# Two of the four sums of weight blocks in the FFN's first product, made by accumulating DMA transfers

## The chip, the core and the metric

The kernel runs on one core of a Trainium2 chip. The metric is device time: the microseconds of one execution of the whole program. Three executions of the kernel before were timed, and one more was taken by the hardware profiler.

## The reference

One layer of a hybrid trunk: 512 latent tokens and 256 context tokens of width 2048 go through a modulated RMS norm, one projection, two groups of heads (a gated token mixer and a bidirectional gated linear attention), an output projection, and a SwiGLU feed-forward network (FFN). Everything is in float32. The change lies in the FFN's first product, `h @ w_in`:

```python
def swiglu(h, w_in, w_out):
    a, b = jnp.split(h @ w_in, 2, axis=-1)
    return (jax.nn.silu(a) * b) @ w_out
...
    f_x = swiglu(modulate(rms_norm(x, g_pre_ffn), mod_x[3], mod_x[4]), w_ffn_in, w_ffn_out)
```

Here h is 512 x 2048 and w_in is 2048 x 11264 (two halves of 5632 columns).

## The kernel before

**Engines and queues.** TensorE multiplies; ScalarE casts, evacuates and evaluates activations; VectorE subtracts and adds; nearly all loads are issued by SyncE (SP) through `load` (L193). GpSimd does 22 small fills in the whole program and issues no transfer. The order of the instructions in each engine's queue is not written out by hand: a scheduler works it out at build time from the dependencies, the program order and its own estimates of what each instruction takes. Every queue then runs strictly in that order, and an instruction whose input is not there holds what is behind it.

**Precision.** A float32 product is made of three matmuls in a reduced format (`three`, L298): each operand is split into a hi part (a cast, ScalarE) and a lo part (source minus hi, VectorE), and hi·hi, hi·lo and lo·hi are summed in PSUM. `parts` (L988) makes both parts of a 128 x 1024 tile, the cast on L992 and the subtraction on L993; three buffers (tags wh, wl) hold them.

**The FFN's first product** is cut into 11 groups of columns (`ffn_group`, L1136), f0 to f10 in the names of the tiles. A group takes 512 columns of each half. The 2 x 2 block product (tokens x depth times depth x column halves) is made with seven products instead of eight, in the manner of Strassen and Winograd: `product(p, q, ...)` (L1118), p = 1 to 7, each over the four quarters q = 0 to 3 of half the depth. One `product` call is 12 matmuls of 512 columns. The left operands (sums of blocks of h, `SP[p][q]`) are made once, before and during group 0, by `make_top` and `make_rest` (L1082, L1089). The right operands are blocks of the weights, `blk(i, j, q, t)` (L1141): half i of the depth, half j of the columns, quarter q, loaded by `wide` (L996) as one transfer of 512 KB, 128 partitions x 1024 floats, in rows of 2 KB.

The stages of a group, by the letter in the names of their hi and lo parts:

- a: blocks (0,0) are loaded into four X tiles (tag X, four buffers) and go into product 1.
- b: blocks (1,0), into R tiles (tag R, four buffers), go into product 2.
- c: blocks (0,1) are loaded into R tiles, VectorE adds each to X[q] (L1169), and the sum goes into product 5.
- d: blocks (1,1) are loaded and added to X[q] (L1174), for product 6.
- e: blocks (1,0) are loaded again and added to X[q] (L1182), for product 4.
- z, y: for each q, block (1,1) is loaded as z and goes into product 3; block (0,1) is loaded as y, VectorE adds z to it (L1191), and the sum goes into product 7. Both are R tiles.

So there are four sums per group, each made four times (q), and all four are made by VectorE: L1169, L1174, L1182 and L1191, 16 adds per group. An R or X tile's buffer is used again when its last reader has finished; the next load into it waits for that. In steady state the hi and lo parts are made some two products ahead of TensorE, as their three buffers come free. Between the stages VectorE combines the accumulators (`vtt`, L1132), and at the end of a group the result is transposed and stored by ScalarE's queue.

During group 0 the pumps `bg` and `bgm` interleave other work: the residual of the mixer (L1034: its RMS, ending in the newton steps of L183 to L185, and the scaling `yo`, L1051) and the operands of the later products (`make_rest`, with the tiles S3 to S7 and h2f).

Of the kernel before, what the change touches and what calls it, by code (L numbers as in the profile page):

```python
# [15 lines left out]
ALU = mybir.AluOpType  # L16
AX = mybir.AxisListType

P = 128
# [72 lines left out]
def trunk_kernel(ctx, tc, cmat, cmask, x, c, ctxt, c_ctx, w_mod, b_mod, g_pre_mix, g_post_mix, g_pre_ffn,  # L92
                 g_post_ffn, w_in, ln_g, ln_b, w_s, b_s, wd2_f, bd_f, wd2_b, bd_b, out_g, w_out, w_ffn_in,
                 w_ffn_out, out):
    nc = tc.nc
    V, S, T, G = nc.vector, nc.scalar, nc.tensor, nc.gpsimd
# [12 lines left out]
    def bank(name, main=True):  # L109
        return pm.tile([P, 512], F32, tag="mm" if main else "ms", bufs=6 if main else 2, name=name)  # L110

    def slot(name, dt=F32, shape=(P, 512)):
        return s2.tile(list(shape), dt, tag="s2", bufs=NS, name=name)
# [26 lines left out]
    def rstd(ss, n, scale, name, eng=None):  # L140

        v = cp.tile([P, n], F32, tag=f"rv{n}", bufs=2, name=name + "v")
        r = cp.tile([P, n], F32, tag=f"rr{n}", bufs=4 if n == 1 else 2, name=name + "r")
        t = cp.tile([P, n], F32, tag=f"rt{n}", bufs=2, name=name + "t")
        V.tensor_scalar(out=v, in0=ss, scalar1=scale, scalar2=EPS, op0=ALU.mult, op1=ALU.add)
        V.tensor_scalar(out=r.bitcast(I32), in0=v.bitcast(I32), scalar1=-0.5, scalar2=float(0x5F3759DF), op0=ALU.mult,
                        op1=ALU.add)
        for _ in range(3):
            if eng is None:
                newton(v, r, t)  # L150
            else:
                eng.tensor_tensor(out=t, in0=r, in1=r, op=ALU.mult)
                eng.tensor_tensor(out=t, in0=t, in1=v, op=ALU.mult)
                eng.tensor_scalar(out=t, in0=t, scalar1=-0.5, scalar2=1.5, op0=ALU.mult, op1=ALU.add)
                eng.tensor_tensor(out=r, in0=t, in1=r, op=ALU.mult)
        return r
# [4 lines left out]
    def rstd_exp(ss, n, name):  # L161

        s1 = cp.tile([P, n], F32, tag=f"s{n}", bufs=4, name=name + "s")
        v = cp.tile([P, n], F32, tag=f"rv{n}", bufs=2, name=name + "v")
        r = cp.tile([P, n], F32, tag=f"rr{n}", bufs=4 if n == 1 else 2, name=name + "r")
        t = cp.tile([P, n], F32, tag=f"rt{n}", bufs=2, name=name + "t")
        V.tensor_reduce(out=s1, in_=ss, axis=AX.X, op=ALU.add)
        S.activation(r, s1, AF.Ln, bias=eps, scale=1.0 / D)
        S.activation(r, r, AF.Exp, scale=-0.5)
        V.tensor_scalar(out=v, in0=s1, scalar1=1.0 / D, scalar2=EPS, op0=ALU.mult, op1=ALU.add)  # L170
        newton(v, r, t)
        return r

    def rstd_sum(ss, name, eng=None):

        s1 = cp.tile([P, 1], F32, tag="s1", bufs=4, name=name + "s")
        V.tensor_reduce(out=s1, in_=ss, axis=AX.X, op=ALU.add)
        return rstd(s1, 1, 1.0 / D, name, eng)
# [102 lines left out]
    def pump():  # L281
        bg.step()
        bgm.step()
# [406 lines left out]
    for o in (0, 512):  # L690
        n = min(512, len(LEVELS) * P - o)
# [260 lines left out]
    for g in range(2):  # L952
# [10 lines left out]
        for b, ev in enumerate(evs):  # L963
            k = g * 4 + b
# [14 lines left out]
    def fslot(name, dt=F32):  # L979
        return fp.tile([P, 512], dt, tag="f", bufs=NF, name=name)  # L980

    def chain_tile(name):
        return st2.tile([P, 1024], F32, tag="X", bufs=4, name=name)

    def raw2(name):
        return st2.tile([P, 1024], F32, tag="R", bufs=4, name=name)

    def parts(src, name):  # L988

        wh = st2.tile([P, 1024], F32R, tag="wh", bufs=3, name=name + "h")  # L990
        wl = st2.tile([P, 1024], F32R, tag="wl", bufs=3, name=name + "l")
        S.copy(wh, src)  # L992
        V.tensor_tensor(out=wl, in0=src, in1=wh.bitcast(F32), op=ALU.subtract)  # L993
        return wh, wl

    def wide(w, r, c0, t, name):  # L996

        load(t.rearrange("p (k c) -> p k c", k=2), w[r:r + 2 * P, c0:c0 + 512].rearrange("(k p) c -> p k c", p=P))
        return t
# [118 lines left out]
    def product(p, q, accs, wp, nq):  # L1118
        hi, lo = SP[p][q]
        for j in range(2):  # L1120
            for t in range(2):
                c = slice(j * 256 + t * P, j * 256 + (t + 1) * P)
                three(accs[t], (hi[:, c], lo[:, c]), cut(wp, j * 512, 512), q == 0 and j == 0, q == nq - 1 and j == 1)

    def two(name):
        return [bank(f"{name}{t}") for t in range(2)]
# [5 lines left out]
    def vtt(out, a, b, op):  # L1132
        for i in range(2):
            V.tensor_tensor(out=out[i], in0=a[i], in1=b[i], op=op)

    def ffn_group(gi):  # L1136
        w, n = w_ffn_in[0], f"f{gi}"
        cols = (gi * 512, HID + gi * 512)
        half_k = D // 2

        def blk(i, j, q, t):  # L1141
            return wide(w, i * half_k + 2 * q * P, cols[j], t, n)

        X = [None] * NQ

        ps = two(n + "p1")
        for q in range(NQ):
            X[q] = blk(0, 0, q, chain_tile(f"{n}X{q}"))
            product(1, q, ps, parts(X[q], f"{n}a{q}"), NQ)
            pump()  # L1150
        u = [fslot(f"{n}u{t}") for t in range(2)]
        for t in range(2):
            S.copy(u[t], ps[t])
        ps = two(n + "p2")
        for q in range(NQ):
            r = blk(1, 0, q, raw2(f"{n}b{q}"))
            product(2, q, ps, parts(r, f"{n}b{q}"), NQ)
            pump()
        a1 = [fslot(f"{n}g{t}") for t in range(2)]
        vtt(a1, ps, u, ALU.add)  # L1160
        for t in range(2):
            S.activation(a1[t], a1[t], AF.Silu)
        if gi == 0:
            bg.drain()

        p5 = two(n + "p5")
        for q in range(NQ):
            r = blk(0, 1, q, raw2(f"{n}c{q}"))
            V.tensor_tensor(out=X[q], in0=X[q], in1=r, op=ALU.add)  # L1169
            product(5, q, p5, parts(X[q], f"{n}c{q}"), NQ)  # L1170
        p6 = two(n + "p6")
        for q in range(NQ):
            r = blk(1, 1, q, raw2(f"{n}d{q}"))
            V.tensor_tensor(out=X[q], in0=X[q], in1=r, op=ALU.add)  # L1174
            product(6, q, p6, parts(X[q], f"{n}d{q}"), NQ)
        vtt(u, u, p6, ALU.subtract)
        u4 = [fslot(f"{n}w{t}") for t in range(2)]
        vtt(u4, p5, u, ALU.add)
        p4 = two(n + "p4")
        for q in range(NQ):  # L1180
            r = blk(1, 0, q, raw2(f"{n}e{q}"))
            V.tensor_tensor(out=X[q], in0=X[q], in1=r, op=ALU.add)  # L1182
            product(4, q, p4, parts(X[q], f"{n}e{q}"), NQ)
        vtt(u, p4, u, ALU.add)

        p7, p3 = two(n + "p7"), two(n + "p3")
        for q in range(NQ):
            z = blk(1, 1, q, raw2(f"{n}z{q}"))
            y = blk(0, 1, q, raw2(f"{n}y{q}"))
            product(3, q, p3, parts(z, f"{n}z{q}"), NQ)  # L1190
            V.tensor_tensor(out=y, in0=y, in1=z, op=ALU.add)  # L1191
            product(7, q, p7, parts(y, f"{n}y{q}"), NQ)
        vtt(u, u, p7, ALU.subtract)
        for t in range(2):
            S.activation(u[t], u[t], AF.Silu)
        b2 = [fslot(f"{n}v{t}") for t in range(2)]
        vtt(b2, p7, u4, ALU.subtract)
        vtt(u4, p3, u4, ALU.subtract)
        vtt(a1, a1, u4, ALU.mult)
        vtt(u, u, b2, ALU.mult)  # L1200
        toks = a1 + u
        for f in range(4):
            ps = bank(f"{n}T{f}", False)
            for t in range(NT):
                T.transpose(ps[:, t * P:(t + 1) * P], toks[t][:, f * P:(f + 1) * P], ident)
            gt = slot(f"{n}t{f}")
            S.copy(gt, ps)
            nc.scalar.dma_start(g_dr[gi * 4 + f], gt)

    for gi in range(HID // 512):  # L1210
        ffn_group(gi)
# [59 lines left out]
    for t in range(NT):  # L1271
# [5 lines left out]
        for cg in range(4):  # L1277
# [3 lines left out]
            f = facc[t][cg]  # L1281
# [4 lines left out]
        r = rstd_exp(fss, 1, f"er{t}")  # L1286
# [32 lines left out]
```

## Time and profile before

| | us |
|---|---|
| median of 3 executions | 2395.07 |
| lowest, highest | 2393.79, 2399.74 |
| the profiled execution, time | 2393.61 |
| its span, first to last instruction | 2391.8 |
| 11 groups of the FFN's first product, in the span | about 980 to 1895 |
| the FFN's second product and the end | about 1885 to 2392 |

The profile is one execution; its time is 1.46 us below the median of the three, and 1.8 us above its own span. Times in the rows are microseconds from the start of the span unless marked ns. PE is TensorE, PEld its weight load, DVE is VectorE, ACT ScalarE, POOL GpSimd, SP SyncE; SPq and ACTq are the instructions by which SP and ScalarE issue a transfer. L1169 is line 1169 of the kernel before. In a row, "out<-in" names the tiles with their buffer numbers left out, "x4" says how many instructions a row stands for, and "[1.00 <-DMA f7y...]" says how long the engine was idle just before and what ended that. "PEclk" is the clock granted to TensorE, where 1.00 is the full 2.4 GHz.

### The profile page before, as it was taken

The page shows a single profiled execution, that of the slowest core. Times are in us where ns is not written, and L with a number is a line of the kernel's source. Part 1 is how long each engine was busy: PE and PEld are TensorE (multiplying, and loading weights), DVE is VectorE, ACT ScalarE, POOL GpSimd, SP SyncE. Part 2 cuts the span into 40 slices and gives each one's busy share as a digit, 9 for nine tenths or more (in the row PEclk, how much of TensorE's full clock was granted, in tenths as well). Part 3 has the DMA queues.
Part 4 walks back from the last instruction along what each step waited for, and adds up shares of the span by engine and source line. Part 5 has one row for each costly group of instructions (what it writes and reads, how often), then busy time and mean ns, then how long its engine had stood idle before and what let it go on. Part 6 is the DMA issues. An engine that isn't in the chain of part 4 may idle for free.

```text
span 2391.8 us, 27761 instructions
## 1 busy us (share of the span) xinstructions
PE 2279.7 (95%) x10386; PEld 1843.2 (77%) x10386; DVE 1595.1 (67%) x2040; ACT 987.8 (41%) x1509; POOL 15.3 (1%) x22
## 2 busy tenths in 40 slices
PE   7999998999996989879999999999999899999998
PEld 2778888788884777658788888888878788888886
DVE  3876577677777766787778778877887632242346
ACT  4443234554564223854434444444444432232232
POOL 0000000000000000000000000000000000000000
PEclk9999999999997999989999999999999999999999
DMA  9967787644435888746576556655666542253344
GB/s 329 338 196 253 248 288 262 223 141 133 132 114 174 308 306 293 239 131 187 176 219 208 190 182 212 212 193 184 203 214 190 170 149 97 97 175 108 106 141 158
DMA packets 244134, 470.99 MB, mean 197 GB/s; under 512 B 20456, under 2 KB 31936, under 8 KB 244000
## 3 DMA queue, kind: packets, MB, share of 16 engines
q1 hardware_dynamic: 233280, 451.49, 58.1%
q10 hardware_dynamic: 10720, 17.74, 2.1%
q8 instruction: 81, 1.33, 0.2%
q14 instruction: 53, 0.43, 0.1%
HBM read 445.04 MB, written 24.13 MB: 196 GB/s over the span
## 4 chain that ended last, share of the span: by engine, by line
PE 64%; DVE 15%; DMA 14%; issue 3%; ACT 3%; SPq 0%; DVEq 0%; ACTq 0%
PE fo L116 18%; PE f7p L116 3%; PE f8p L116 3%; PE f5p L116 3%; PE f4p L116 3%; PE f0p L116 2%; PE g0a L116 2%; PE u1a L116 2%; PE fz L116 2%; PE vv1a L116 2%; PE cv L116 2%; PE wo L116 2%; PE f2p L116 2%; PE k L116 2%; PE v1a L116 2%
## 5 line engine op out<-in xcount | busy, mean ns | idle before, releaser
L1224 DVE TENSOR_TENSOR gl<-gr,gh 128x512 fp32r<-128x512 f32 x44 | 28.4, 687 | 28.9 <-ACT gh L1223 28.9
L1223 ACT CAST gh<-gr 128x512 fp32r<-128x512 f32 x44 | 25.1, 618 | 32.8 <-DMA gr<-g_dr 25.9
L229 DVE SCALAR_TENSOR_TENSOR m50acc<-m50w,cpair,m50acc 128x1024 f32<-128x1024 f32 x16 | 20.5, 1282 | 13.6 <-DMA m50w<-in_w_mod_dram 13.5
L832 ACT ACTIVATE lv<-lv 128x1024 f32<-128x1024 f32 x20 | 21.0, 1055 | 19.5 <-DVE lv L831 19.5
L993 DVE TENSOR_TENSOR fo_2l<-fo_r,fo_2h 128x1024 fp32r<-128x1024 f32 x8 | 9.8, 1225 | 28.4 <-ACT fo_2h L992 28.4
L993 DVE TENSOR_TENSOR fo_0l<-fo_r,fo_0h 128x1024 fp32r<-128x1024 f32 x8 | 9.8, 1224 | 26.8 <-ACT fo_0h L992 26.8
L116 PE MATMUL vv0a<-vv_0h,hxh 128*128 128x512 f32 x64 | 27.6, 430 | 0.0
L116 PE MATMUL fo<-fo_0h,gh 128*128 128x512 f32 x64 | 25.8, 403 | 1.7 <-ACT gh L1223 1.7
L993 DVE TENSOR_TENSOR fo_18l<-fo_r,fo_18h 128x1024 fp32r<-128x1024 f32 x8 | 9.8, 1226 | 25.8 <-ACT fo_18h L992 25.8
L116 PE MATMUL vv1a<-vv_0h,hxh 128*128 128x512 f32 x64 | 27.0, 422 | 0.0
L833 DVE TENSOR_TENSOR lv<-lv,kq 128x1024 f32<-128x1024 f32 x20 | 24.4, 1220 | 3.8 <-ACT lv L832 3.8
L1283 ACT ACTIVATE junk<-fc 128x512 bf16<-128x512 f32 x16 | 10.1, 631 | 40.4 <-DVE fc L1282 40.3
L116 PE MATMUL g0a<-hxh,g_0h 128*128 128x512 f32 x64 | 26.7, 418 | 0.0
L116 PE MATMUL g1a<-hxh,g_0h 128*128 128x512 f32 x64 | 26.4, 412 | 0.3 <-ACT g_0h L277 0.3
L116 PEld LDWEIGHTS s<-lv 128*128 128x128 f32 x192 | 24.9, 191 | 2.1 <-issue 0.5
L993 DVE TENSOR_TENSOR fo_8l<-fo_r,fo_8h 128x1024 fp32r<-128x1024 f32 x8 | 9.8, 1226 | 25.0 <-ACT fo_8h L992 25.0
L993 DVE TENSOR_TENSOR fo_10l<-fo_r,fo_10h 128x1024 fp32r<-128x1024 f32 x8 | 9.8, 1224 | 24.9 <-ACT fo_10h L992 24.9
L116 PE MATMUL v1a<-v_0h,hxh 128*128 128x512 f32 x64 | 26.3, 412 | 0.0
L993 DVE TENSOR_TENSOR fo_12l<-fo_r,fo_12h 128x1024 fp32r<-128x1024 f32 x8 | 9.8, 1225 | 24.8 <-ACT fo_12h L992 24.8
L993 DVE TENSOR_TENSOR fo_14l<-fo_r,fo_14h 128x1024 fp32r<-128x1024 f32 x8 | 9.8, 1226 | 24.6 <-ACT fo_14h L992 24.6
L229 DVE SCALAR_TENSOR_TENSOR m51acc<-m51w,cpair,m51acc 128x1024 f32<-128x1024 f32 x16 | 20.5, 1283 | 8.5 <-DMA m51w<-in_w_mod_dram 8.2
L993 DVE TENSOR_TENSOR fo_16l<-fo_r,fo_16h 128x1024 fp32r<-128x1024 f32 x8 | 9.8, 1224 | 24.5 <-ACT fo_16h L992 24.5
(3877 smaller groups left out, 7993.4 us busy)
## 6 DMA issues: line engine op xcount, KB each, us to landing
fo_r<-in_w_ffn_out_dram SPq DMA_DIRECT2D x80, 512.0 KB
gr<-g_dr SPq DMA_DIRECT2D x22, 512.0 KB
mx4w<-in_w_mod_dram SPq DMA_DIRECT2D x16, 512.0 KB
mx8w<-in_w_mod_dram SPq DMA_DIRECT2D x16, 512.0 KB
mx12w<-in_w_mod_dram SPq DMA_DIRECT2D x16, 512.0 KB
mc4w<-in_w_mod_dram SPq DMA_DIRECT2D x16, 512.0 KB
mc8w<-in_w_mod_dram SPq DMA_DIRECT2D x16, 512.0 KB
mc12w<-in_w_mod_dram SPq DMA_DIRECT2D x16, 512.0 KB
```

What stands on the lines that cost most here:

```text
L116: return T.matmul(o, lhsT=l, rhs=r, start=start, stop=stop)
L229: ins = V.scalar_tensor_tensor(out=acc, in0=raw[:, j].rearrange("p i c -> p (i c)"), scalar=cvec[:, k0 + j:k0 + j + 1], in1=acc, op0=ALU.m ...
L832: S.activation(lv, lv, AF.Exp)
L833: V.tensor_tensor(out=lv, in0=lv, in1=kq[h], op=ALU.mult)
L993: V.tensor_tensor(out=wl, in0=src, in1=wh.bitcast(F32), op=ALU.subtract)
L1223: S.copy(hi, r[:, j * 512:(j + 1) * 512])
L1224: V.tensor_tensor(out=lo, in0=r[:, j * 512:(j + 1) * 512], in1=hi.bitcast(F32), op=ALU.subtract)
L1283: S.activation(junk, f, AF.Square, accum_out=fss[:, cg:cg + 1])
```

## The change

Two of the four sums are made by DMA transfers that add what they fetch to what is already in the destination. They are issued by GpSimd. For c, the block (0,1) is no longer loaded into an R tile; a transfer adds it to X[q] directly. For y, the block (0,1) is loaded into y as before, and a second transfer fetches the block (1,1) from HBM once more and adds it to y; z, with the same block, is still loaded for product 3. VectorE's adds of L1169 and L1191 go; those of d and e stay.

```diff
         def blk(i, j, q, t):
             return wide(w, i * half_k + 2 * q * P, cols[j], t, n)
 
+        def add_blk(i, j, q, t):
+
+            r = i * half_k + 2 * q * P
+            nc.gpsimd.dma_start(t.rearrange("p (k c) -> p k c", k=2),
+                                w[r:r + 2 * P, cols[j]:cols[j] + 512].rearrange("(k p) c -> p k c", p=P),
+                                accum_op=ALU.add)
+
         X = [None] * NQ
...
         p5 = two(n + "p5")
         for q in range(NQ):
-            r = blk(0, 1, q, raw2(f"{n}c{q}"))
-            V.tensor_tensor(out=X[q], in0=X[q], in1=r, op=ALU.add)
+            add_blk(0, 1, q, X[q])
             product(5, q, p5, parts(X[q], f"{n}c{q}"), NQ)
...
             z = blk(1, 1, q, raw2(f"{n}z{q}"))
             y = blk(0, 1, q, raw2(f"{n}y{q}"))
             product(3, q, p3, parts(z, f"{n}z{q}"), NQ)
-            V.tensor_tensor(out=y, in0=y, in1=z, op=ALU.add)
+            add_blk(1, 1, q, y)
             product(7, q, p7, parts(y, f"{n}y{q}"), NQ)
```

## Rows read from the trace of the kernel before

**Rows 1.** The page's first part: busy time, share of the span and instructions of each engine.

```profile
PE 2279.7 (95%) x10386; PEld 1843.2 (77%) x10386; DVE 1595.1 (67%) x2040; ACT 987.8 (41%) x1509; POOL 15.3 (1%) x22
```

**Rows 2.** Windows: start and end, length, busy us of each engine, then clock, DMA share, GB/s.

```profile
core 0: us, PE busy (x) PEld busy (x) DVE busy (x) ACT busy (x) POOL busy (x), PEclk, DMA share, GB/s
1003.00:1021.00 18.00, 9.72 (x39) 6.43 (x37) 16.99 (x24) 13.00 (x24) 0.00 (x0) 0.74 0.78 247
...
1095.00:1890.00 795.00, 789.56 (x3517) 642.05 (x3516) 618.60 (x620) 348.32 (x380) 0.00 (x0) 1.00 0.62 196
1630.00:1645.00 15.00, 15.00 (x68) 12.43 (x67) 9.37 (x10) 6.24 (x6) 0.00 (x0) 1.00 0.56 167
```

**Rows 3.** Waits of TensorE, 1095 to 1895 us: waiter, releaser, total, times, longest.

```profile
PE f1p L116 <- DVE f1e0l L993: 1.0, 1, 1.0
PE f9p L116 <- DVE f9e0l L993: 0.9, 1, 0.9
PE f1p L116 <- DVE f1b1l L993: 0.8, 1, 0.8
...
PE f9p L116 <- DVE f9y2l L993: 0.3, 1, 0.3
...
PE f8p L116 <- DVE f8b1l L993: 0.2, 1, 0.2
```

**Rows 4.** The chain of waits in group 0, 1000 to 1062 us: start, duration, work.

```profile
1004.30 1.14 DVE f0X L1169
...
1007.91 1.14 DVE f0X L1169
...
1009.12 1.13 DVE f0X L1169
...
1015.37 1.14 DVE f0X L1169
...
1059.10 1.22 DVE f0y L1191
```

**Rows 5.** VectorE's instructions in order of time, group 7: start, duration, instruction, idle before.

```profile
1615.37 1.23 DVE L1191 TENSOR_TENSOR f7y<-f7y,f7z 128x1024 f32<-128x1024 f32 x1 [1.00 <-DMA f7y<-in_w_ffn_in_dram]
...
1617.65 1.22 DVE L993 TENSOR_TENSOR f7e0l<-f7X,f7e0h 128x1024 fp32r<-128x1024 f32 x1
...
1634.04 1.23 DVE L1191 TENSOR_TENSOR f7y<-f7y,f7z 128x1024 f32<-128x1024 f32 x1 [1.81 <-DMA f7y<-in_w_ffn_in_dram]
1635.18 1.22 DVE L993 TENSOR_TENSOR f7y1l<-f7y,f7y1h 128x1024 fp32r<-128x1024 f32 x1
...
1640.25 1.23 DVE L1191 TENSOR_TENSOR f7y<-f7y,f7z 128x1024 f32<-128x1024 f32 x1 [2.58 <-DMA f7y<-in_w_ffn_in_dram]
```

**Rows 6.** The last subtraction of stage a and the last cast of stage c, group 7.

```profile
1579.26 1.22 DVE L993 TENSOR_TENSOR f7a3l<-f7X,f7a3h 128x1024 fp32r<-128x1024 f32 x1
...
1599.95 1.05 ACT L992 CAST f7c3h<-f7X 128x1024 fp32r<-128x1024 f32 x1
```

**Rows 7.** SP's loads of y2 and y3 of group 7; a load of c in group 1 and its add.

```profile
1629.53 0.37 SPq L195 DMA_DIRECT2D f7y<-in_w_ffn_in_dram  x1
...
1636.42 0.37 SPq L195 DMA_DIRECT2D f7y<-in_w_ffn_in_dram  x1
...
1104.37 0.37 SPq L195 DMA_DIRECT2D f1c<-in_w_ffn_in_dram  x1
...
1109.89 1.23 DVE L1169 TENSOR_TENSOR f1X<-f1X,f1c 128x1024 f32<-128x1024 f32 x1 [5.54 <-DMA f1c<-in_w_ffn_in_dram]
```

**Rows 8.** Group 7: casts of y1 and y2, subtraction of y2 (ns), TensorE's reads of y2l, y3l.

```profile
1632.63 1.05 ACT L992 CAST f7y1h<-f7y 128x1024 fp32r<-128x1024 f32 x1 [1.66 <-PE f7p L116]
...
L992 ACT CAST f7y2h<-f7y x1: 1053/1053/1053, 1638.1 to 1638.1; 128x1024 fp32r<-128x1024 f32 x1
...
L116 PE MATMUL f7p<-f7y2l,S7h x4: 389/389/389, 1643.5 to 1645.6; 128*128 128x512 f32 x4
L993 DVE TENSOR_TENSOR f7y2l<-f7y,f7y2h x1: 1218/1218/1218, 1641.4 to 1641.4; 128x1024 fp32r<-128x1024 f32 x1
...
L116 PE MATMUL f7p<-f7y3l,S7h x4: 389/389/389, 1649.0 to 1651.0; 128*128 128x512 f32 x4
```

**Rows 9.** The page's third part, SP's queue: packets, MB, share of 16 engines' span.

```profile
q1 hardware_dynamic: 233280, 451.49, 58.1%
```

**Rows 10.** A fill on GpSimd: line, tile, shape, count, busy us, mean ns, idle before.

```profile
L221 POOL MEMSET mx8acc<- 128x1024 f32 x1 | 1.0, 961 | 0.0
```

## The prediction, made blind

> **What bounds the kernel now.** The page's first part comes first: TensorE is busy 95% of the span [rows 1]; what can be won is where it is not. The windows say where: in the eleven groups that the change touches, once they run steadily (1095 to 1890 us), TensorE is idle 795.0 - 789.56 = 5.4 us in all, while VectorE is busy 78% and the DMA engines 62%; in the first group (1003 to 1021 us) TensorE is idle almost half of the time and VectorE is the busy one, 16.99 of 18 us [rows 2]. TensorE's own waits in the steady part are then read by name: ten rows, 4.7 us together, all on the lo halves e0l, b1l and one y2l of VectorE [rows 3]. Last, the chain of waits of the first group: four of the adds that go (L1169) lie on it, 1.14 us each, and one of L1191 [rows 4].
>
> **What the change takes off VectorE.** 11 groups x 8 adds of 1.22 us [rows 5] go, 107 us of an engine that is mostly not the limit. Two places count.
>
> In the first group VectorE sets the pace between 1003 and 1021 us. The four adds of L1169 on the chain are 1.14 + 1.14 + 1.13 + 1.14 = 4.5 us [rows 4], and what follows on the chain (the newton steps, yo, the S5 parts that TensorE waits for) is queued behind them. I take 4.5 us. The ends: 0, where ScalarE becomes the limit, and all eight adds, 9.1 us; the one of L1191 at 1059 us is left to the range.
>
> In the steady groups the add y0 (L1191) stands ahead of e0l in VectorE's order and waits for the load of y: in group 7 it starts at 1615.37 after 1.00 us of waiting, and e0l at 1617.65 [rows 5]; in the same way the first add of L1169 stands ahead of b1l and waits for the load of c. With the adds gone VectorE waits for neither. I take the 4.7 us of [rows 3]; the ends are 0 and the 5.4 us that TensorE is idle there [rows 2]. Together **-9.2 us**.
>
> **The c sums (L1168 and L1169): hidden.** GpSimd may issue c{q} as soon as the casts of phase a have read X[q]. In group 7 the last of them, a3l, ends at 1579.26 + 1.22 = 1580.5, and the cast that needs X[3] + c runs at 1599.95 [rows 6]: 19.4 us of cover. No load in this stretch needs that long: the slowest that I found was issued at 1104.37 and its add began at 1109.89, so 5.5 us [rows 7], and twice that is still covered. GpSimd has nothing else to do here, so the queue that this moves to is empty, and SP's loses four issues of 0.37 us per group; the four R buffers that held c also come free, so d is fetched earlier. Nothing of this is on the path: 0.
>
> **The y sums (L1191): the risk.** Here the order changes. Before, y was loaded, and z, which product 3 needs anyway, was added to it. Now y must land first, then GpSimd fetches the same block (1, 1) a second time and adds it into y: one more transfer in series, 4 more loads of 512 KB per group. Nothing waits behind it on GpSimd but the next such transfer and the next group's c0, which isn't free before that group's a0 is cast. ScalarE's cast of y2 stands ahead of z3's in its queue, so a late y2 holds both and TensorE with them.
>
> How much time has it? For y0 and y1 plenty: their buffers come free in phase e, and y0 landed at 1615.37 [rows 5]. y2 is the tight one, since it gets its buffer only when y0 is released: its load is issued at 1629.53 [rows 7], its add begins on landing at 1634.04 [rows 5], and TensorE takes y2l at 1643.5. Cast (1.053) and subtract (1.218) must fit before [rows 8], so the sum has to be there by 1641.2: a **budget of 7.2 us**. y3 landed at 1640.25 [rows 5] and must be there by 1649.0 - 2.3 = 1646.7 [rows 8]: 6.5 us, but its load waits for y1's release, and y1l stood behind the add that waited until 1634.04 [rows 5], which goes; y1's cast was done at 1633.7 [rows 8], so y3 is issued about 1.5 us sooner, 8.0 us.
>
> How long does an accumulating transfer take? The trace has none; call it L, from y's landing to the sum's. **Lower end:** the fastest load of its size, y3, 1636.42 to 1640.25, 3.8 us [rows 5, 7]. **Upper end:** the slowest, 5.5 us [rows 7], twice over, because two operands are read: 11.0 us. **Value:** y2's own load, 4.5 us; plus the transfer part once more for the second operand, 0.581 x 2391.8 us / 451.49 MB x 0.524 MB = 1.6 us [rows 9]; plus 0.6 us for GpSimd being slower to issue than SP, by its nearest row, a memset of 0.96 us [rows 10] against SP's 0.37. That is 6.7 us, nearer to the plain loads because the queues are not full: the DMA engines are busy 56% between 1630 and 1645 us [rows 2]. 6.7 lies 0.5 us inside the budget, so I take a stall of 0. The margin is thin.
>
> The Trainium skill, page "DMA: Bandwidth & Descriptors" (Anatomy of one DMA, SWDGE path), fits a transfer issued by GpSimd as 2.0 us + bytes / 436 GB/s; as an estimate that is 3.2 us for this one, and no run here shows it. By it the stall is 0 too, with 4 us to spare. It describes a transfer with the engines to itself; here even a plain load takes 3.8 to 5.5 us, so I hold to the rows.
>
> Traffic as a bound: per group 28 loads of 512 KB and four stores of 256 KB now take a share of 0.62; 4 more loads and 8 second reads are at most 12 x 1.6 us = 19 us more in the 795 / 10 us of a group, 0.62 + 0.24 = 0.86 [rows 2, 9]. Not full, so transfers grow longer but don't become the limit.
>
> **The sum:** 0 for c, 0 for y, -9.2 for VectorE. From the profiled execution's 2393.61 us that is 2384.4; the median of the runs is 1.46 us higher, and on its scale 2395.07 - 9.2 = **2385.9 us**. A difference of 0.3% (7.2 us) is about what can be told from none.
>
> **Rival 1, slower: y2 arrives after its budget.** Each of the eleven groups stalls TensorE L - 7.2 us at product 7, q 2 (later in the group nothing gives it back). This takes the gain away at L = 7.2 + 9.2 / 11 = 8.0, and makes the kernel slower by over 0.3% from 8.7. If all of a load's 4.5 us doubled, L = 9.0 and the stall 11 x 1.8 = 20 us: 2395.07 - 9.2 + 19.8 = 2405.7; at 11.0, 11 x 3.8 = 42 us: 2427.7. For it: 0.5 us of margin on a price that no row shows, and SP's loads of the next group's X and b share the DMA engines. Against it: the 56%, and a budget of 1.6 plain loads. The Trainium skill, page "Collectives: The Full Stack" (The bandwidth ceiling), says that an adding transfer reads two sources through one ring and so runs at half the rate: its rule, applied to the whole 4.5 us, is the 2405.7 case; no run here shows it yet.
>
> **Rival 2, no change: the gain isn't there.** In the first group ScalarE's casts and TensorE's transposes are interleaved with VectorE's adds, and what the adds free may be waited for elsewhere; in the steady groups the small waits may move to another lo half. Then 2391 to 2396. For it: none of the 4.7 us is longer than 1.0 us. Against it: in the first group four adds stand one after another on the chain.
>
> **Rival 3, no change: GpSimd is held up by VectorE.** If GpSimd can't write its transfer's commands while VectorE runs, it loses up to one instruction, 1.22 us [rows 5]: L = 7.9, a stall of 11 x 0.7 = 7.7 us, 2393.6. The Trainium skill, page "SBUF — State Buffer" (SBUF: two separate sides), knows this trap for VectorE's two-port modes alone and exempts two-input adds; the rows of VectorE here are all such adds and subtracts, so I give it little.
>
> **How the numbers follow.** Forecast 0.47 (0.40 of it past 0.3%), rival 1 0.29, rival 2 0.14, rival 3 0.10. Faster 0.40; within 0.3% 0.07 + 0.14 + 0.10 = 0.31; slower 0.29. The likeliest case's own range is 2380 to 2392: its low end is 2395.07 - 9.1 - 5.4. The 8-in-10 range runs from 2380 to 2413, which is L = 9.7; above that lies about a tenth, and a little below 2380.
>
> **What would show it.** Right: the waits on e0l and b1l are gone; the first group's c0 product starts 4 to 5 us earlier; TensorE waits for no cast of y2 or y3; GpSimd's transfers for y land within 7 us. Wrong: TensorE's list of waits is headed by ScalarE's y2h and y3h, about eleven times each, released by the accumulating transfer (rival 1), or the first group runs as long as before (rival 2). If GpSimd's queue issues c later than the casts of phase a allow, or c's casts wait for it, the 0 for c is wrong.

## The result, and the profile after

The changed kernel takes 2416.76 us (median of seven, 2404.36 to 2434.19) against 2393.97 us (median of seven, 2392.19 to 2399.74) of the kernel before: a ratio of 1.0101 [1.0066, 1.0136], **1.0% slower**. The prediction was 2385.9 us, range 2380 to 2413. The profiled execution is the longest of the seven, 2434.19 us, so its trace shows the loss somewhat larger than the median.

The page of the kernel after, its first part and the two queues that the change touches (columns as in [rows 1, 9]):

```profile
PE 2299.4 (95%) x10386; PEld 1857.8 (76%) x10386; DVE 1507.1 (62%) x1952; ACT 983.9 (40%) x1509; POOL 121.8 (5%) x110
...
q1 hardware_dynamic: 221312, 428.42, 53.6%
q0 software_dynamic: 23936, 46.14, 11.2%
```

VectorE's 88 adds are gone and 88 transfers have moved to GpSimd. TensorE's busy time has grown by 19.7 us over [rows 1] with the same number of matmuls: a first sign that matmuls ran slower, and not only later.

TensorE's waits of the kernel after in the steady groups (waiter, releaser, total, times, longest):

```profile
PE f4p L116 <- ACT f4y2h L992: 3.3, 1, 3.3
PE f10p L116 <- ACT f10y3h L992: 2.8, 1, 2.8
PE f2p L116 <- ACT f2y2h L992: 2.4, 1, 2.4
PE f5p L116 <- ACT f5y3h L992: 1.9, 1, 1.9
PE f3p L116 <- ACT f3y2h L992: 1.8, 1, 1.8
PE f9p L116 <- ACT f9y3h L992: 1.7, 1, 1.7
PE f6p L116 <- ACT f6y3h L992: 1.7, 1, 1.7
PE f7p L116 <- ACT f7y3h L992: 1.4, 1, 1.4
PE f1p L116 <- ACT f1y2h L992: 1.2, 1, 1.2
...
PE f8p L116 <- ACT f8y2h L992: 0.5, 1, 0.5
```

The waits on e0l and b1l of [rows 3] have left the list. In all ten steady groups TensorE now waits once for ScalarE's cast of y2 or of y3, and then for the subtraction behind it, for up to 0.8 us more. Group 0 waits as well, 2.6 us for its y2. Rival 1's sign is there, with one difference: it is one late cast in a group, y2's or y3's, and which of the two changes from group to group.

What releases that cast is read in the chain of waits of the kernel after, group 2 (start, duration, work):

```profile
1235.70 8.80 DMA f2y<-in_w_ffn_in_dram
...
1244.60 1.06 ACT f2y1h L992
...
1245.69 1.24 DVE f2y1l L993
...
1247.01 8.75 DMA f2y<-in_w_ffn_in_dram
...
1255.85 1.05 ACT f2y2h L992
...
1256.93 1.24 DVE f2y2l L993
...
1258.21 4.21 PE f2p L116 x9
```

Two accumulating transfers, 8.80 and 8.75 us, stand on the chain where the kernel before had adds of 1.2 us. The same stretch in the timeline of the kernel after, SP's, GpSimd's and TensorE's instructions (start, duration, instruction, idle before):

```profile
1240.61 0.37 SPq L195 DMA_DIRECT2D f2y<-in_w_ffn_in_dram  x1
...
1247.01 1.20 POOL L1147 DMA_DIRECT2D f2y<-in_w_ffn_in_dram  x1 [10.11 <-DVE f2y1l L993]
...
1254.16 0.39 PE L116 MATMUL f2p<-f2z2h,S3l 128*128 128x512 f32 x1
1256.95 0.79 PE L116 MATMUL f2p<-f2y2h,S7h 128*128 128x512 f32 x1 [2.40 <-ACT f2y2h L992]
1258.21 0.80 PE L116 MATMUL f2p<-f2y2l,S7h 128*128 128x512 f32 x1 [0.46 <-DVE f2y2l L993]
```

From the issue of y2's own load to the start of GpSimd's transfer it is 1247.01 - 1240.61 = 6.4 us, where the prediction took 4.5 to the start of VectorE's add [rows 5, 7]; the sum takes another 8.8 us. (The row names the subtraction f2y1l as what ended GpSimd's wait. The trace's completion times put the end of y2's load at 1246.44, and in the forty sums of groups 1 to 10 GpSimd starts 0.56 us or more after the load is complete, with a median of 0.56 too; so the wait was for the load, and that f2y1l ended then is taken for a coincidence.) TensorE has nothing from 1254.55 to 1256.95, and 0.46 us again. The first matmul after the gap is marked 0.79 us long, twice the 0.39 before it. The windows of the same stretch show why (columns as in [rows 2], with the granted clock third from the end):

```profile
1249.00:1252.00 3.00, 3.00 (x15) 2.49 (x14) 0.00 (x0) 0.00 (x0) 0.84 (x1) 1.00 1.06 251
...
1254.00:1256.00 2.00, 0.55 (x3) 0.13 (x1) 0.00 (x0) 0.15 (x1) 0.00 (x0) 1.00 1.12 215
1256.00:1258.00 2.00, 0.79 (x1) 0.29 (x1) 1.07 (x1) 1.84 (x2) 0.00 (x0) 0.71 0.34 60
1258.00:1260.00 2.00, 1.79 (x4) 1.50 (x5) 1.66 (x3) 1.05 (x1) 0.00 (x0) 0.50 0.31 46
1260.00:1262.00 2.00, 2.00 (x6) 1.53 (x5) 0.86 (x1) 0.00 (x0) 0.00 (x0) 0.50 0.96 342
1262.00:1264.00 2.00, 2.00 (x6) 1.57 (x6) 0.00 (x0) 0.69 (x1) 0.00 (x0) 0.59 0.97 358
1264.00:1266.00 2.00, 2.00 (x10) 1.63 (x9) 1.23 (x1) 0.36 (x1) 0.09 (x1) 1.00 0.14 52
...
1101.30:1927.00 825.70, 799.76 (x3510) 650.00 (x3508) 536.77 (x538) 342.81 (x379) 95.56 (x79) 0.98 0.81 213
```

Two things are to be seen. From 1249 to 1256, the larger part of y2's sum, the DMA engines are fully taken (the rows shown have 1.06 and 1.12; a packet's whole time is counted in the window in which it starts, so a share can pass 1). Over the whole sum, 1247.00 to 1255.75, the share is 0.95, where the mean of the groups is 0.81. And after the gap the granted clock is 0.50, the level of 1.2 GHz, until past 1263. Against full speed that lacks 2 x (0.29 + 0.50 + 0.50 + 0.41) = 3.4 us, beside the 2.9 us idle. The last row is the whole stretch from the first matmul of group 1 to the start of the last product of group 10: 825.7 us, against 793.4 in the kernel before (its row stands with the experiments).

### The profile page after: what moved, and what is told of

Its sections match the earlier page's. It is cut to its first block, busy times and chain, and to the rows that moved or that the text cites. A ratio compares the mean times of both kernels' runs of the same rounds, so it can differ in the third digit from the quotient of the medians.

```text
span 2432.4 us, 27928 instructions
## 1 busy us (share of the span) xinstructions
PE 2299.4 (95%) x10386; PEld 1857.8 (76%) x10386; DVE 1507.1 (62%) x1952; ACT 983.9 (40%) x1509; POOL 121.8 (5%) x110
## 3 DMA queue, kind: packets, MB, share of 16 engines
q1 hardware_dynamic: 221312, 428.42, 53.6%
q0 software_dynamic: 23936, 46.14, 11.2%
## 4 chain that ended last, share of the span: by engine, by line
PE 73%; DMA 14%; DVE 7%; ACT 4%; issue 2%; SPq 0%; ACTq 0%; DVEq 0%; POOLq 0%
PE fo L116 18%; PE f1p L116 3%; PE f9p L116 3%; PE f4p L116 3%; PE f5p L116 3%; PE f3p L116 3%; PE f6p L116 3%; PE f10p L116 2%; PE f7p L116 2%; PE f8p L116 2%; PE f2p L116 2%; PE k L116 2%; PE g0a L116 2%; PE u1a L116 2%; PE fz L116 2%
## 5 line engine op out<-in xcount | busy, mean ns | idle before, releaser
L116 PE MATMUL vv0a<-vv_0l,hxh 128*128 128x512 f32 x64 | 26.1, 408 | 0.0
L116 PE MATMUL v1a<-v_0l,hxh 128*128 128x512 f32 x64 | 25.8, 404 | 0.1
L116 PE MATMUL vv0a<-vv_0h,hxl 128*128 128x512 f32 x64 | 25.9, 405 | 0.0
L116 PE MATMUL g1a<-hxl,g_0h 128*128 128x512 f32 x64 | 25.8, 403 | 0.0
L116 PE MATMUL v1a<-v_0h,hxl 128*128 128x512 f32 x64 | 25.7, 401 | 0.0
L116 PE MATMUL g0a<-hxh,g_0l 128*128 128x512 f32 x64 | 25.6, 399 | 0.0
```

What stands on the lines that cost most here:

```text
L116: return T.matmul(o, lhsT=l, rhs=r, start=start, stop=stop)
```

## The experiments

The theory was rival 1: the sum of y arrives after TensorE has run out of work, in y2 and y3 alone, and the sums of c are a small gain. Against it stood that the traffic as a whole, or GpSimd's issues, slow everything; and of the late sum it was open whether reading a second operand, the source in HBM, or y's late buffer makes it late. All ratios are to the kernel before, run beside it on the same chip.

**Only the sums of c by transfer.** The sum of y goes back to VectorE:

```diff
-            add_blk(1, 1, q, y)
+            V.tensor_tensor(out=y, in0=y, in1=z, op=ALU.add)
```

> Only the c sum is made by the accumulating transfer; VectorE adds z to y again. Theory LATE (all of the loss is that y2 or y3 arrives after its cast could run, and TensorE then stands still and goes on at half clock): nothing of it is left here, and the gain of the c adds is: waits of TensorE on b1l gone, the first group shorter; 2384 to 2391 us against about 2394. Rival TRAFFIC (the loss is in the added traffic and in transfers issued by GpSimd as such): c's transfers read X as well and share the queues, so part of the loss stays, above 2396. Rival NO GAIN (what VectorE is freed from is waited for elsewhere): 2392 to 2396.

2381.56 us, ratio 0.9959 [0.9943, 0.9974]: faster by 10.6 us against the 2392.12 beside it. The sums of c are hidden, and they carry the gain.

**Only the sums of y by transfer.** c is loaded and added by VectorE, as before:

```diff
-            add_blk(0, 1, q, X[q])
+            r = blk(0, 1, q, raw2(f"{n}c{q}"))
+            V.tensor_tensor(out=X[q], in0=X[q], in1=r, op=ALU.add)
```

> Only the y sum is made by the accumulating transfer; VectorE adds c to X again. Theory LATE: the whole loss is here, one stall of TensorE on y2h or y3h per group and a stretch at half clock behind it; 2405 to 2440 us, and slower than the changed kernel by what c gave it, 0 to 6 us. Rival TRAFFIC: half of the transfers are gone, so about half of the loss of 23 us: near 2405. If c is what costs, this one comes out near 2394.

2415.29 us, ratio 1.0098 [1.0076, 1.0121]: the loss is y's. It comes with a lower DMA share than the changed kernel has (0.75 against 0.81), so the traffic as a whole does not explain it. TensorE's longest waits in the steady groups of this run, others being 0.8 us and less:

```profile
PE f8p L116 <- ACT f8y2h L992: 1.9, 1, 1.9
PE f7p L116 <- ACT f7y2h L992: 1.5, 1, 1.5
PE f3p L116 <- ACT f3y2h L992: 1.4, 1, 1.4
```

The two halves do not add up: -10.6 us for c alone and +23.2 us for y alone make +12.6, and the changed kernel lost 22.8. The scatter of the changed kernel allows that much, but the traces point the same way: from the issue of the late y's load to its cast it is 13.1 us at the median of the ten steady groups here, and 14.6 in the changed kernel. So the transfers of c, harmless by themselves, seem to make those of y later; that is not shown by a run of its own.

**c, and y0 and y1, by transfer; y2 and y3 by VectorE.**

```diff
-            add_blk(1, 1, q, y)
+            if q < 2:
+                add_blk(1, 1, q, y)
+            else:
+                V.tensor_tensor(out=y, in0=y, in1=z, op=ALU.add)
```

> c and the first two y sums (q 0 and 1) by transfer, y2 and y3 by VectorE. Theory LATE: y0 and y1 have some 13 us to land, the transfers take 6 to 9, so nothing stalls and the waits on e0l and b1l are gone: 2383 to 2390 us, the fastest of the four. Rival TRAFFIC: 22 of the 44 added loads are there, so about half of the loss stays: 2400 to 2408. Rival NO GAIN: 2392 to 2396.

2385.19 us, 0.9965 [0.9951, 0.9979]. Half of the sums of y move without harm: only y2 and y3, whose buffers come free late, cost anything. They bring nothing measurable beyond c alone either.

**y ahead of z.** Everything is as in the change, but y is loaded and summed before z is loaded, so y takes the buffer that z of the same q had:

```diff
-            z = blk(1, 1, q, raw2(f"{n}z{q}"))
             y = blk(0, 1, q, raw2(f"{n}y{q}"))
-            product(3, q, p3, parts(z, f"{n}z{q}"), NQ)
             add_blk(1, 1, q, y)
+            z = blk(1, 1, q, raw2(f"{n}z{q}"))
+            product(3, q, p3, parts(z, f"{n}z{q}"), NQ)
             product(7, q, p7, parts(y, f"{n}y{q}"), NQ)
```

> As the changed kernel, but in each q the load of y and its accumulating transfer are written ahead of the load of z, so that y gets the buffer that comes free first, one product (2.7 us) sooner. Theory LATE: the budget of y2 grows from 7.2 to about 9.9 us, more than most of the transfers take, so most stalls go: 2386 to 2402 us. z then has one product less, with a plain load of 4 to 5 us, which is enough. Rival TRAFFIC: the same transfers, so the same time as the changed kernel, 2405 to 2435.

2381.35 us, 0.9963 [0.9947, 0.9979]: with the same 88 accumulating transfers the loss of 1.0% turns into a gain of 0.4%. Its timeline, group 2:

```profile
1223.46 0.37 SPq L195 DMA_DIRECT2D f2y<-in_w_ffn_in_dram  x1
...
1228.44 1.20 POOL L1147 DMA_DIRECT2D f2y<-in_w_ffn_in_dram  x1 [12.88 <-DMA f2y<-in_w_ffn_in_dram]
...
1236.36 1.05 ACT L992 CAST f2y2h<-f2y 128x1024 fp32r<-128x1024 f32 x1 [3.31 <-DMA f2y<-in_w_ffn_in_dram]
...
1239.96 0.39 PE L116 MATMUL f2p<-f2y2h,S7h 128*128 128x512 f32 x1
```

The sum takes 7.9 us here against 8.8 in the same group of the changed kernel (7.3 against 8.2 at the median of the steady groups), and y's load 5.0; the cast ends 1240.0 - 1237.4 = 2.6 us before TensorE takes it. From the issue of y2's load to TensorE's first use of y2 there are 1239.96 - 1223.46 = 16.5 us here. In the changed kernel it was 1256.95 - 1240.61 = 16.3 with TensorE's wait of 2.4 in it, so 13.9 without. The transfer has not become fast, its start has become early.

**The loss and its parts.** The same stretch (first matmul of group 1 to the start of the last product of group 10) in the windows of the kernel before, of c alone, and of y ahead of z, one fence each:

```profile
1095.10:1888.50 793.40, 787.96 (x3509) 640.72 (x3509) 618.42 (x619) 347.27 (x379) 0.00 (x0) 1.00 0.62 196
```

```profile
1090.00:1873.50 783.50, 783.00 (x3510) 642.14 (x3509) 582.28 (x579) 346.40 (x379) 47.24 (x39) 1.00 0.71 199
```

```profile
1091.00:1875.50 784.50, 783.32 (x3510) 642.04 (x3509) 539.32 (x539) 344.84 (x379) 95.52 (x79) 1.00 0.84 225
```

Between the changed kernel and y ahead of z lie 825.7 - 784.5 = 41.2 us for the same instructions. TensorE is idle 825.70 - 799.76 = 25.9 us in the one and 1.2 us in the other; and in windows of 1 us, one minus the granted clock adds up to 13.7 us in the one and to 0.0 in the other. These two, 24.7 + 13.7 = 38.4 us, are nearly all of it. This trace is of the changed kernel's longest execution. In that of y alone, which lost about what the changed kernel lost at its median, the stretch is 13 us longer than before, with 13.1 us of idle time and 5.1 us of half clock; group 0 is 4.0 us longer. The DMA share is higher in the faster of the two, 0.84 against 0.81.

**A plain copy in the place of the sum.** GpSimd fetches the same bytes into y without adding, so the sum of y is left out:

```diff
-                                accum_op=ALU.add)
+                                **({'accum_op': accum} if accum else {}))
...
-            add_blk(1, 1, q, y)
+            add_blk(1, 1, q, y, None)
```

> As the changed kernel, but the second transfer for y only copies block (1, 1) over y and adds nothing (the sum of y is left out, so product 7 has another operand; the work of every engine stays). It measures what the adding costs against the path through GpSimd. Theory SECOND READ (the adding transfer is long because it reads two operands, 3.1 us of the DMA engines against 1.6): from issue to landing falls from 8.1 to about 6.5 us, most stalls go, 2384 to 2400 us. Rival PATH (the time lies in GpSimd's issue of 1.2 us and in landing): 8 us as before and 2405 to 2435 us.

2388.26 us, 0.9977 [0.9961, 0.9992]: with as many transfers and the same bytes, the whole loss is gone. It is not the same transfer less the adding, though: GpSimd's own part is 0.73 us here and 1.20 for a sum, and there are fewer packets, 144 in a copy (it and the sums of c make 18304 together) and 272 in a sum (23936 / 88). Its GpSimd queue on the page (packets, MB, share of 16 engines), and GpSimd's issues and landing times of y in the tile view of group 2:

```profile
q0 software_dynamic: 18304, 46.14, 8.7%
```

```profile
L1147 POOL DMA_DIRECT2D f2y<-in_w_ffn_in_dram x4: 722/730/753, 1212.9 to 1242.1; - x4
...
DMA to landing us min/median/max: 4.0/6.7/7.6
```

and the tile view of y of group 2 in the kernel after:

```profile
L1147 POOL DMA_DIRECT2D f2y<-in_w_ffn_in_dram x4: 1203/1203/1203, 1225.0 to 1251.2; - x4
...
DMA to landing us min/median/max: 7.3/8.8/10.2
```

Over groups 1 to 10 the medians lie between 4.8 and 6.7 us for the copy and between 6.2 and 8.8 for the sum. The queue rows give the price on the engines: 0.112 x 2432.4 us / 46.14 MB x 0.524 MB = 3.1 us per sum, against 0.536 x 2432.4 / 428.42 x 0.524 = 1.6 us per plain load. In the copy's run, where half of the queue's transfers (those of c) still add, it is 0.087 x 2387.2 / 46.14 x 0.524 = 2.4 us, the middle of 1.6 and 3.1. So adding costs a second transfer's time, about 1.5 us on 16 engines, and some 2 us until landing, of which GpSimd's longer issue is 0.5. With these 2 us y2 or y3 is late in every steady group. Without them TensorE still waits eight times for y2l, 0.3 to 0.8 us each: even the copy is barely in time.

**Adding from z in SBUF instead of HBM.**

```diff
-            add_blk(1, 1, q, y)
+            nc.gpsimd.dma_start(y, z, accum_op=ALU.add)
```

> As the changed kernel, but the transfer adds the tile z that is already in SBUF to y, and does not fetch the block from HBM again. Theory LATE with SECOND READ: two operands are still read, y still has to land first and z too, so y2 and y3 stay late: 2400 to 2430 us, somewhat better since the loads lose 44 neighbours in HBM. Rival TRAFFIC in HBM (the 44 added loads are what makes it late): 2382 to 2392.

2409.21 us, 1.0056 [1.0039, 1.0073]. The landing time falls by about one microsecond, to some 7.1 us, of which 0.3 us is GpSimd's shorter issue (0.86 us). By the medians 22.8 - 16.5 = 6.3 us of the loss go, but the two intervals overlap, so not even these are certain. Most of the loss stays without the second fetch from HBM, and it went with the copy, which does fetch: where the source lies matters less than that there is a second operand. Its tile view of y, group 2:

```profile
DMA to landing us min/median/max: 6.5/6.8/7.2
```

**The kernel before with y ahead of z.** Without any accumulating transfer, to see whether the order brings something by itself:

```diff
-            z = blk(1, 1, q, raw2(f"{n}z{q}"))
             y = blk(0, 1, q, raw2(f"{n}y{q}"))
+            z = blk(1, 1, q, raw2(f"{n}z{q}"))
```

> The kernel before, VectorE making all four sums, with the load of y written ahead of that of z. A control for the run with y ahead of z: if the order of the two loads is worth something by itself, it shows here. Theory LATE: nothing waits for y long enough in the kernel before, so 2391 to 2396, no change. Rival ORDER (the gain of that run came from the order): 2380 to 2386.

2391.37 us, 0.9992 [0.9976, 1.0008]: nothing that can be told.

**Only y by transfer, y ahead of z**, c on VectorE (the edit of y alone and that of y ahead of z together):

> Only the y sum by the accumulating transfer, y loaded ahead of z; VectorE adds c to X. Theory LATE: no stall on y, and the waits on e0l, which stood behind the add of y0, are gone, while those on b1l stay: 2384 to 2391 us. If the gain comes from c alone: 2392 to 2396.

2391.94 us, 0.9989 [0.9974, 1.0005], just above what was expected: a miss. In its profiled execution group 10 begins 710.1 us after group 1, against 716.5 before, a gain of 6.4 us that the ten timed executions do not confirm. What the removal of y's adds is worth alone stays open between nothing and these few microseconds.

**One more R buffer.** The order is as in the change; the pool of R tiles has five buffers in the place of four. Two of the kernel's 29 half-size buffers of tag f go to make room:

```diff
-NF = 29
+NF = 27
...
-        return st2.tile([P, 1024], F32, tag="R", bufs=4, name=name)
+        return st2.tile([P, 1024], F32, tag="R", bufs=5, name=name)
```

> As the changed kernel, in its own order of z and y, but with five R buffers instead of four (and 27 instead of 29 buffers of the pool f, to make room). y2 then gets the buffer that z0 gives back, one product (2.7 us) ahead of y0's. Theory LATE: a budget of some 9.9 us again, as with y ahead of z, so the stalls go without any change of order: 2380 to 2390 us. Rival (the order of the transfers on the queues is what helped, not the time): 2400 to 2430.

2378.14 us, 0.9950 [0.9923, 0.9977], the lowest median of all, and it beats both kernels; its interval overlaps with those of c alone and of y ahead of z. A lead over these two is not to be seen in the steady groups: from the first matmul of group 1 to that of group 10 it takes 710 us, against 708 with c alone and 709 with y ahead of z. Its timeline, group 2:

```profile
1218.73 0.37 SPq L195 DMA_DIRECT2D f2y<-in_w_ffn_in_dram  x1
...
1223.88 1.20 POOL L1147 DMA_DIRECT2D f2y<-in_w_ffn_in_dram  x1 [13.23 <-DMA f2y<-in_w_ffn_in_dram]
...
1232.38 1.05 ACT L992 CAST f2y2h<-f2y 128x1024 fp32r<-128x1024 f32 x1 [4.05 <-DMA f2y<-in_w_ffn_in_dram]
...
1235.23 0.39 PE L116 MATMUL f2p<-f2y2h,S7h 128*128 128x512 f32 x1
```

Here 5.2 us of load and 8.5 us of sum end early enough for the cast to be done 1.8 us ahead of TensorE. An edit that touches neither the transfers nor their number nor their order in the code removes the loss: y's late buffer is the cause, the slow sum the condition. (What two buffers of f less do by themselves was not tried.)

**All four sums by transfer**, y ahead of z:

```diff
-            r = blk(1, 1, q, raw2(f"{n}d{q}"))
-            V.tensor_tensor(out=X[q], in0=X[q], in1=r, op=ALU.add)
+            add_blk(1, 1, q, X[q])
...
-            r = blk(1, 0, q, raw2(f"{n}e{q}"))
-            V.tensor_tensor(out=X[q], in0=X[q], in1=r, op=ALU.add)
+            add_blk(1, 0, q, X[q])
```

> y ahead of z, and now all four sums (c, d, e and y) by accumulating transfers; VectorE makes none. Theory LATE with SECOND READ: d and e have about 11 us between the last read of X[q] and the cast of the sum, the transfers take 8, so each alone fits; but the DMA engines, busy 82% with two sums, get 8 more second reads per group, 8 x 1.55 = 12 us in 79, which makes 0.98: the transfers grow longer and TensorE waits for X, 2395 to 2440 us. Rival (they still fit, VectorE freed gives nothing more): 2380 to 2388.

2388.66 us, 0.9988 [0.9973, 1.0003], between the two expectations. VectorE's adds are all gone, but the DMA engines are nearly full:

```profile
1100.00:1880.00 780.00, 772.27 (x3431) 627.23 (x3431) 431.28 (x443) 334.32 (x367) 189.08 (x156) 1.00 0.95 223
```

TensorE is idle 7.7 us of 780 again, most of it in waits of up to 0.8 us on e and y, and the gain is given back. Waits this short left the granted clock at 1.00.

## Why the prediction was wrong

**The step that failed** is "6.7 lies 0.5 us inside the budget, so I take a stall of 0". Both sides of that comparison were off.

- *The sum, L = 6.7 us.* Measured from GpSimd's start: a median of about 8.2 us over the steady groups, 5.7 at best; the sums that TensorE waited for took 7.3 to 9.1. Of the 1.5 us missing, GpSimd's issue has 0.2 (1.20 us instead of the 0.96 taken from a fill), and the second operand nothing: its price was put at 1.6 us and measured as 3.1 - 1.6 = 1.5. The rest, about 1.3 us, is put down to the load on the DMA engines: 4.5 us was a load's time in the traffic of the kernel before, and the 56% of [rows 2] a mean of that traffic, while in group 2 the sum ran at a share of 0.95. The copy, which adds nothing, bears this out: 6.05 us at its median, 1.2 us more than 4.5 and GpSimd's issue make. One term was put at nothing without a reason: L counts from y's landing, and GpSimd starts 0.56 us after it, where VectorE's adds that waited for y started 0.12 us after it (median). These 0.44 us are nearly the margin of 0.5 us.
- *The budget, 7.2 us for y2 and 8.0 for y3.* It held y's own load at 4.5 us, and y3's 1.5 us sooner. In the changed kernel loads of y2 took 4.1 to 7.0 us and loads of y3 4.2 to 7.1, to GpSimd's start. This came with y's own sums: up to completion alone the loads of y have a median of 3.8 us before, 3.9 with c alone and 5.1 here. In group 2 that took 6.4 - 4.5 = 1.9 us out of 7.2. Load and sum had 4.5 + 7.2 = 11.7 us together and took 15.2; the cast was 3.5 us late by this, and TensorE stood idle for 2.9.
- *The price of lateness.* Rival 1 named the mechanism and its place, and had 0.29. But its formula at the measured L gives 11 x (8.2 - 7.2) - 9.2 = +1.8 us, and about +7 with the 0.44 us by which GpSimd starts later after landing than VectorE's add did, not +22.8: it holds the budget fixed, and it prices a stall at its length alone. The half clock after most of the longer stalls adds 13.7 us to 25.9 us of idle time (in the longest execution). The tail of the range, 2413, was made by that formula, and so it lay 4 us short of the median.

**The sums of c: right.** No cast of c waited for a transfer (the closest landed 5.4 us ahead of its cast), and the waits on b1l are gone, although the slowest of these transfers took 13.5 us, far above the 5.5 us I looked at: the cover of 19.4 us [rows 6] was large enough to bear that error.

**VectorE, -9.2 us: about the right size, the wrong split, so in part luck.** c alone gains 10.6 us. Predicted were 4.5 us in group 0 and 4.7 in the steady groups. From the first matmul of group 0 to that of group 1 it is 114.6 us before, 114.5 with c alone and between 111.4 and 112.7 with c and a harmless y: 0.1 to 3.2 us. In the changed kernel it is 118.1, with the wait for y2 in it. The sign for group 0, a c0 product 4 to 5 us earlier, came out at 2.3 us there and 1.4 with c alone. The windows of group 0, of the kernel before and of c alone, show what became of the rest (columns as in [rows 2]):

```profile
980.50:1095.10 114.60, 93.39 (x383) 70.07 (x382) 92.81 (x120) 67.24 (x111) 0.00 (x0) 0.91 0.50 152
```

```profile
975.50:1090.00 114.50, 96.60 (x384) 73.15 (x383) 88.73 (x116) 67.33 (x111) 4.85 (x4) 0.87 0.55 155
```

TensorE's idle time falls from 21.2 to 17.9 us, but the mean granted clock falls from 0.91 to 0.87, which takes these 3.3 us back. The steady part from the first matmul of group 1 to that of group 10, here in the kernel before and with c alone, one fence each,

```profile
L116 PE MATMUL f1p<-f1a0h,S1h x4: 389/389/389, 1095.1 to 1097.2; 128*128 128x512 f32 x4
...
L116 PE MATMUL f10p<-f10a0h,S1h x4: 389/389/389, 1811.6 to 1813.6; 128*128 128x512 f32 x4
```

```profile
L116 PE MATMUL f1p<-f1a0h,S1h x4: 389/389/389, 1090.0 to 1092.0; 128*128 128x512 f32 x4
...
L116 PE MATMUL f10p<-f10a0h,S1h x4: 389/389/389, 1797.6 to 1799.7; 128*128 128x512 f32 x4
```

shrinks from 1811.6 - 1095.1 = 716.5 us to 1797.6 - 1090.0 = 707.6: 8.9 us, more than the 5.4 us of idle time that I called an end. The windows above show where it hid: with c alone TensorE's idle time falls from 5.4 to 0.5 us and its *busy* time from 787.96 to 783.00, for the same matmuls. Short stalls had been counted as busy; that the modelled ends of matmuls hide them is argued, not shown.

**Rival 3: no sign of it where it would have counted.** For the sums of y GpSimd's issue took 1203 to 1222 ns, beside a VectorE 65% busy (536.77 of 825.7 us). For those of c it took 1203 to 1542, and nothing waited for them. **Rival 2** described y's part: removing y's adds brought nothing that the times can tell.

**The rules beside the rows.** The sum occupies the DMA engines 3.1 us against 1.6 for a plain load of its size. The Trainium skill, page "Collectives: The Full Stack" (The bandwidth ceiling), gives the adding step of a collective half the rate of a copying one, for its two source reads. The trace agrees in the time on the engines, with a factor of 1.94; until landing a sum took 8.2 us and a copy 6.05, a factor of 1.4. The Trainium skill, page "DMA: Bandwidth & Descriptors" (Anatomy of one DMA), has the fit that gave 3.2 us as an estimate for the whole transfer, and does not say there what else ran. The fastest sum measured took 5.7 us and the fastest plain copy by GpSimd 4.0, so for these kernels the measurement decides against it. I had weighed these two rightly, and still put rival 1 at 0.29, since I let 0.5 us of margin on an unmeasured price decide the sign.

## What to carry to other kernels

A transfer put in series behind another is to be held against the whole way from the release of its buffer to the first reader, with both transfers at the duration that they take under the new traffic, and the load looked at in the burst where they run, not as a mean. Where it comes out close, give it an earlier buffer, by order or by one more buffer: that turned the same transfers from +1.0% into -0.4 to -0.5%. Move only what the cover can bear: the sums with 19 us of cover were free, all four filled the DMA engines and gave the gain back.

## What the runs showed of the hardware that was not expected

- After 2.4 us without work in group 2 TensorE ran at the granted clock 0.50 (1.2 GHz) for 3.4 / 0.50 = 6.8 us. In group 1 of the same trace a wait of 1.2 us was followed by 3.4 us at 0.50; in group 6 one of 1.7 us left the clock at 1.00. In the kernels whose waits in the steady groups stayed at 0.8 us and below, the granted clock stayed at 1.00 there.
- Issuing one of these transfers takes GpSimd 1.20 us (0.73 for a plain copy, 0.86 where it adds from SBUF), against 0.37 us on SP. GpSimd starts 0.56 us after the load that it waits for is complete.
- The changed kernel scatters by 1.2% (2404 to 2434 us) where the kernel before, beside it, scatters by 0.3% (by 0.7% in the widest of the other comparisons). In its trace it varies from group to group whether y2 or y3 is the late one; that the same holds between executions is likely, but only one was traced.
